# Arena places on multiples of 256 bytes in a two-batch hybrid encoder layer

## The chip, the cores and the metric

The kernel runs on one core of one Trainium2 chip. The metric is device time in microseconds (us), the median of three runs. The engines are called PE (TensorE, matmuls), PEld (its weight load), DVE (VectorE), ACT (ScalarE), POOL (GpSimd) and SP (SyncE, which here issues DMAs). SBUF addresses are bytes within one partition.

## What is computed

One encoder layer is applied to two batches with the same weights: A (1024 tokens) and B (512 tokens), 1024 channels, fp32.

```
h = RMSNorm(x);  p = h @ w_in      # q|k, v, o, z, gates | 3 x (q, k, v), z | merge gates
y_A = o * headnorm(h_fwd + h_bwd) * silu(z_A)    # mLSTM, 4 heads x 256, both directions, chunks of 128
y_B = (weighted mix of 3 dilation groups) * silu(z_B)   # 3 x 8 heads x 64, banded windows with a bias
merged = sig(g_A) * (y_A @ w_proj_m) + sig(g_B) * (y_B @ w_proj_a)
x + RMSNorm(merged @ w_out)
```

## The kernel before, in words

Every fp32 matrix is split into a high and a low part (fp32r), and a product is made of three matmuls, hi·hi (L209), hi·lo (L210) and lo·hi (L211), all in `mm3`. A dense matmul has 128 x 128 weights and 512 moving columns.

**Stage 1 (0 to 966 us)** is the input projection of A. Half blocks of h, split, lie in tiles Hh0 to Hh6 and Hl0 to Hl6; products `d` use them with weight pairs phla and phlb (`unit_pair`). The last products are the merge gates (columns `c`), which ACT writes out to gt_a. At the end the x of B (tiles xs) is normalised and turned into H (`short_input`, L313 and L319).

**Stage 2 (966 to 2260 us)** has a pool `arena` with one tile per place, taken by name with `take` (L252): H0 to H3, X0, X1, Q0, Q1, K0, K1, V0a, V0b, V1a, V1b, each 2048 fp32 per partition, the V places 2064 (eight chunks of 258: 256 values and two columns of ones). The order in which the places are first taken, the loop over names in `body`, is their order in memory. Taking a place that lies over tiles of stage 1 makes its first writer wait for their last reader. The mixer stages share the places one after another:

- mlstm of A (966 to 1312): q and k of a head in Q0/K0 or Q1/K1, v in V0a, V0b or V1a, V1b, X as work space. `ml_load` queues the loads; `fetch` (L248 to 250) issues them on SP.
- attend of A (1312 to 1640): queries in Q, keys in the V places; the `lg` matmuls (L1362, and L210/L211 in `mm3`) have 256 columns.
- mlstm of B with the combine of A beside (1640 to 1825), attend of B (1825 to 2095), combine of B and the rest (2095 to 2260).

While a mixer waits for its vector work, PE is filled with dense units of 512-column matmuls (`Fill`, in the counts STEPS): first the input projection of B (`short_units`, 768 steps), then `branches` and `final` of (A,0), (A,1) and (B,0), where the second figure is the half of the tokens. `branches` of (A,0) and (B,0) keep the split rows in V0b (hi), V1b (lo) and K0 (hi), K1 (lo): they are moving operand in `proj_m` (w_pm is the weight), are then overwritten with the merged rows by `proj_a`, and those are the weights in `final` (w_out moving). For (A,1) the same rows lie in H0 to H3, and V1b and K1 hold the attention's rows, moving operand in `proj_a`. `place` (L1569) names these places.

Weights come through a ring: a DMA into wraw (`load_w`, L261), ACT's copy to the high part (wh, L272), DVE's or POOL's difference to the low part (wl, L278). When the mixers no longer need them, X0 and Q1 serve as more of these pairs. DMAs are issued by SP in the mlstm stages and by POOL in the attend stages. The order of PE and SP in stage 2 is written out by hand; on DVE, ACT and POOL a scheduler sets it.

The gates of the mLSTM are summed into a table `gall` (128 x 128). `gate_tile` (L916) makes it, clears it on POOL, and makes the small tiles col and gb beside it. For A the table lies in a pool of stage 1; for B it lies in the pool `gates` behind the arena from the start of stage 2. B's gates are written to it (ACT, L815) while attend of A runs, and `lanes` (L934) transposes it there.

Of the kernel before, what the change touches and what calls it, by code (L numbers as in the profile page):

```python
# [22 lines left out]
F32 = mybir.dt.float32  # L23
# [6 lines left out]
P = 128  # L30
# [83 lines left out]
class Fill:  # L114
# [27 lines left out]
    def weights(self, first=True):  # L142

        if first:
            self.base = self.taken
        self.taken += 1
        self.load()
        if self.taken == len(self.ready):
            self.net.rest()
        return self.ready[self.taken - 1]  # L150
# [31 lines left out]
class Net:  # L182
# [68 lines left out]

    def take(self, name, dt=F32R, cols=2048):  # L252

        width = 2064 if name[0] == "V" else 2048
        return self.arena.tile([P, width], F32R, name=name, bufs=1)[:, :cols].bitcast(dt)

    def load_w(self, src, kt=KT, cols=P):
# [655 lines left out]

        return T.gall.rearrange("p (j r) -> p j r", r=32)[:, :, :4 * T.n].rearrange("p j (h c) -> p j h c", c=T.n)[:, :, :, t]

    def gate_tile(self, T, pool, first):  # L916
        T.gall = first.tile([P, P], F32, name=f"gall{T.S}")
        self.nc.gpsimd.memset(T.gall, 0.0)
        T.col = pool.tile([P, 3, 64], F32, name=f"col{T.S}")
        T.gb = pool.tile([P, 1], F32, name=f"gb{T.S}")  # L920
        self.nc.sync.dma_start(T.gb, self.a[f"gb{T.n}"])
# [647 lines left out]
    def place(self, which, i, dt=F32R):  # L1569

        return self.take((("V0b", "V1b", "K0", "K1"), ("H0", "H1", "H2", "H3"))[which][i], dt).rearrange("p (k t) -> p k t", k=4)
# [182 lines left out]
def body(tc, a):  # L1754
    N = Net(tc, a)
    nc = tc.nc
    (x1, y1), (x2, y2) = a["runs"]
    with ExitStack() as st:
        st.enter_context(tc.manual_schedule(engines={mybir.EngineType.PE}))
        pool = lambda name, bufs, **kw: st.enter_context(tc.tile_pool(name=name, bufs=bufs, side="left", **kw))  # L1760
        N.const = pool("const", 1)
        N.dram = dram = st.enter_context(tc.tile_pool(name="dram", bufs=1, space=DRAM))
        A = Tokens(dram, 1024, a[x1], a[y1], "a")
        B = Tokens(dram, 512, a[x2], a[y2], "b")
# [6 lines left out]
        with ExitStack() as s1:  # L1771
            hp = N.pool(s1, "H", 1, "left")
# [3 lines left out]
            with ExitStack() as sv:  # L1776
                vw = N.pool(sv, "vw", 1, "left")
                us = N.pool(s2, "us", 1, "right")
                s3, s4 = ExitStack(), ExitStack()
                begin = [vw.tile([P, 4 * VW], F32R, name=x, bufs=2) for x in ("vhi", "vlo")], *N.value_weights(vw)  # L1780
                r = [us.tile([P, 6], F32, name=f"xr{t}") for t in range(6)]
                one = us.tile([P, VW], F32, name="u2", bufs=4)[0:1, :P]
                diag = [us.tile([P, VW], F32, name="u2b", bufs=4)[:, :P] for _ in range(4)]
                xp = N.pool(s3, "x0", 1, "left"), N.pool(s4, "x1", 1, "right")
                xt = [[xp[i].tile([P, D], F32, name=f"x{i}{t}") for t in range(4)] for i in range(2)]
                minus = H[1][T4][:, 3, :P]
                spare = H[0][T4].bitcast(F32).rearrange("p a c -> p (a c)")
                row, pw = spare[0:1, D:], spare[:, :D]
                rows = lambda i, t: nc.sync.dma_start(xt[i][t], A.x[i * BLK + t * P:i * BLK + (t + 1) * P])
                weights = lambda j, kh: nc.sync.dma_start(begin[1 + j][:, kh], a["w_vp"][0, j, kh])  # L1790
                nc.scalar.dma_start(row, a["prew"][0:1])
                nc.scalar.dma_start(N.prew, a["prewc"])
                for t in range(4):
                    rows(0, t)
                weights(0, 0)
                for t in range(4):
                    rows(1, t)
                for j, kh in ((0, 1), (1, 0), (1, 1)):
                    weights(j, kh)
                nc.vector.memset(one, 1.0)  # L1800
                for i in range(2):
                    p = ps.tile([P, BLK], F32, name="d")
                    nc.tensor.matmul(p, one, row[:, i * BLK:(i + 1) * BLK], start=True, stop=True)
                    nc.vector.tensor_copy(pw[:, i * BLK:(i + 1) * BLK], p)
                nc.scalar.activation(minus, N.ident, AF.Copy, scale=-1.0)
                opened = []

                def co():
                    if not opened:
                        s4.close()  # L1810
                        opened.append(N.pool(s2, "co", 1, "right"))
                    return opened[0]

                def again():
                    H[0][T4] = place("h", T4)

                turns = N.combos(ps, H, xt, r, H[1][T4][:, :2].rearrange("p a c -> p (a c)"), pw, minus, again, diag)
                values = [N.value_group(0, A, H, vw, us, co, ps, None, (*begin, turns), [x[:, :VW] for x in xt[0]])]
                next(values[0])
                N.small(N.const)  # L1820
                N.gate_tile(A, N.const, hp)
                for _ in values[0]:
                    pass
                s3.close()
                more, turn = N.pool(sv, "more", 1, "left"), itertools.cycle(range(5))
                values += [N.value_group(g, A, H, vw, us, co, ps, late if g == 3 else None, more=more, turn=turn)
                           for g in range(1, 4)]
                next(values[1])
                with ExitStack() as s4:
                    lanes = N.lanes(A, N.pool(s4, "lane", 1, "right"), lambda: ps.tile([P, BLK], F32, name="d"))  # L1830
                    for g in range(1, 3):
                        for j, _ in enumerate(values[g]):
                            if j % 3 == 0:
                                with tc.issue_after(N.splits[0].ins), tc.issue_after(N.splits[1].ins):
                                    next(lanes, None)
                    for _ in lanes:
                        pass
                    with tc.issue_after(N.splits[0].ins):
                        N.halved()
                    N.bias_tables(N.pool(s4, "tab", 1, "right"), ps, dram)  # L1840
                for _ in range(7):
                    next(values[3])
# [63 lines left out]
        with ExitStack() as s1:  # L1906
# [4 lines left out]
            N.wsplit = [[ring.tile([P, RING], F32R, name=f"w{x}{i}") for x in "hl"] for i in range(3)]  # L1911
            N.arena = N.pool(s1, "arena", 1, "left")
            gb = N.pool(s1, "gates", 1, "left")
            N.gate_tile(B, gb, gb)
            short = N.short_units(B)
            N.last = (B, 0)
            finals = [N.final(*x) for x in ((A, 0), (A, 1), (B, 0))]
# [11 lines left out]
                end = N.short_input(N.pool(s2, "turn", 6, "right", PSUM), xt)  # L1929
            with tc.issue_after(end.ins):  # L1930
                gate(0, 6, c)
            for x in ("X0", "X1", "Q1", "K1", "V1a", "V1b", "Q0", "K0", "V0a", "V0b"):
                N.take(x)
            keep.close()
            kept = {}
# [6 lines left out]
            with ExitStack() as s2:  # L1942
                sp = N.pool(s1, "sp", 1, "right")
                N.sw = Rot(N, [sp.tile([P, BLK], F32R, name=f"sw{i}") for i in range(4)])
                N.sraw = sp.tile([P, BLK + 2], F32, name="sraw")
                nc.gpsimd.memset(N.sraw, 0.0)
                N.sg = Rot(N, [sp.tile([P, BLK], F32R, name="sg")])
                ym = N.pool(s2, "ym", 1, "right")
                N.ym_of = Rot(N, [ym.tile([P, 256], F32, name=f"ym{i}") for i in range(2)])
                N.lasting = (N.sw, N.sg, N.ym_of)  # L1950
                N.mlstm(A, fill, STEPS[0], N.ml_load(A, 0), ("a", "num", "kv"), 4,
                        hold("qkv", lambda: N.att_load(A, 0)))
                N.side = nc.gpsimd
                with ExitStack() as s3:
                    lanes = N.lanes(B, N.pool(s3, "lane2", 1, "right"), lambda: N.bank("o").rearrange("p a b -> p (a b)"))
                    N.attend(A, fill, STEPS[1], kept["qkv"], ("pt", "o", "lg"), 10, hold("head", lambda: N.ml_load(B, 0)),
                             lanes, range(44, 96, 10))
                    for _ in lanes:
                        pass
                    N.close()  # L1960
                N.side = nc.sync
                assert len(N.wsplit) == 3
                with ExitStack() as s3:
                    small = N.pool(s3, "mix", 1, "right")
                    azs = [small.tile([P, BLK], F32, name=f"az{i}") for i in range(2)]
                    beside = N.combine(A, lambda: N.ml_ps.tile([P, 4, P], F32, name="a"), ("V0b", "V1b"), ("K0", "K1"), small, azs, True)
                    N.mlstm(B, fill, STEPS[2], kept["head"], ("kv", "num", "a"), 1,
                            hold("qkv", lambda: N.att_load(B, 0)), beside)
                    for _ in beside:
                        pass  # L1970
                    N.flush(lambda p: True)
                fill.until(SHORT)
# [78 lines left out]
```

## Time and profile before

| what | value |
|---|---|
| median of 3 runs | 2256.57 us (2256.50 to 2256.66) |
| span of the profiled execution | 2259.7 us |
| granted PE clock | 1.00 |
| PE busy in mlstm A, 966 to 1312 us | 343.5 of 346 us |
| PE busy in attend A, 1312 to 1640 us | 327.8 of 328 us |
| PE busy in mlstm B, 1640 to 1825 us | 184.3 of 185 us |
| PE busy in attend B, 1825 to 2095 us | 268.5 of 270 us |
| PE busy in the rest, 2095 to 2260 us | 158.3 of 165 us |

The profiled execution lies 3.1 us above the median of the runs. In a group of instructions the columns are: line, engine, operation, output<-inputs, partitions x elements, count, then busy us in total, the mean ns of one, and the idle time before them. Buffer numbers are left out of the names, so K is K0 or K1, and wh any of the ring's high parts. A matmul's time in such a row runs from its start to its modelled end, and consecutive matmuls overlap.

### The profile page before, as it was taken

How to read it: one execution, taken by the hardware profiler on the slowest of the kernel's cores; microseconds unless marked ns; L12 is line 12 of the kernel's file. 1: busy time of each engine (PE TensorE's matmuls, PEld its weight loads, DVE VectorE, ACT ScalarE, POOL GpSimd, SP SyncE). 2: the span in 40 equal slices, each digit the busy share in tenths (PEclk: the TensorE clock that was granted, in tenths of full speed). 3: DMA queues.
4: the chain of work that ended last, by engine and by line, in shares of the span. 5: the costliest groups of instructions: out<-in, count | busy, mean ns of one | idle time of the engine just before them, and what ended most of it. 6: DMA issues, size and time to landing. Idle time of an engine off the chain costs nothing.

```text
span 2259.7 us, 35388 instructions
## 1 busy us (share of the span) xinstructions
PE 2244.2 (99%) x12226; PEld 1964.6 (87%) x12226; DVE 1509.5 (67%) x2875; ACT 1129.2 (50%) x2369; POOL 718.6 (32%) x1000
## 2 busy tenths in 40 slices
PE   9999999999999999999999999999999999999998
PEld 8999888888888888888888899999888888888887
DVE  7765577687776556558887755544689844655674
ACT  6432244344444434357777655566665644554332
POOL 1000333333333223237676610011165522221221
PEclk9999999999999999999999999999999999999999
DMA  3652455543332223284664789997678797776663
GB/s 123 168 134 76 172 205 192 192 176 121 112 111 103 84 84 140 103 298 153 226 223 127 191 217 235 253 245 221 203 248 284 238 278 211 233 251 200 233 230 109
DMA packets 222685, 418.27 MB, mean 185 GB/s; under 512 B 24841, under 2 KB 128969, under 8 KB 222506
## 3 DMA queue, kind: packets, MB, share of 16 engines
q1 hardware_dynamic: 194536, 315.86, 44.4%
q0 software_dynamic: 24368, 87.56, 12.4%
q10 hardware_dynamic: 3602, 12.59, 1.4%
q8 instruction: 97, 1.59, 0.3%
q14 instruction: 82, 0.67, 0.1%
HBM read 296.19 MB, written 128.12 MB: 188 GB/s over the span
## 4 chain that ended last, share of the span: by engine, by line
PE 95%; DMA 2%; issue 1%; ACT 1%; POOL 1%; DVE 0%; DVEq 0%; SPq 0%; POOLq 0%; ACTq 0%
PE d L211 14%; PE d L209 14%; PE d L210 14%; PE dense L209 12%; PE dense L211 12%; PE dense L210 12%; PE o L1398 4%; PE pt L1385 2%; PE lg L1362 2%; PE num L211 1%; PE num L209 1%; PE num L210 1%; PE kv L209 1%; PE a L1070 1%; PE kv L210 1%
## 5 line engine op out<-in xcount | busy, mean ns | idle before, releaser
L209 PE MATMUL dense<-H,wh 128*128 128x512 f32 x664 | 270.6, 408 | 0.8 <-DVE V0b L1643 0.8
L211 PE MATMUL dense<-H,wl 128*128 128x512 f32 x664 | 260.9, 393 | 0.0
L210 PE MATMUL dense<-H,wh 128*128 128x512 f32 x664 | 260.2, 392 | 0.0
L210 PE MATMUL d<-Hl,phla 128*128 128x512 f32 x608 | 236.5, 389 | 0.0
L211 PE MATMUL d<-Hh,phla 128*128 128x512 f32 x608 | 236.5, 389 | 0.0
L209 PE MATMUL d<-Hh,phla 128*128 128x512 f32 x608 | 236.5, 389 | 0.0
L278 DVE TENSOR_TENSOR wl<-wraw,wh 128x1024 fp32r<-128x1024 f32 (+1 forms) x121 | 149.3, 1234 | 70.0 <-ACT wh L272 69.9
L1374 DVE CUSTOM_DVE_ANT_0 ls<-lg,bias 128x256 f32<-128x256 f32 (+1 forms) x288 | 93.7, 362 | 132.8 <-PE lg L1362 71.2
L211 PE MATMUL d<-Hh,phlb 128*128 128x512 f32 x456 | 177.4, 389 | 0.0
L209 PE MATMUL d<-Hh,phlb 128*128 128x512 f32 x456 | 177.4, 389 | 0.0
L210 PE MATMUL d<-Hl,phlb 128*128 128x512 f32 x456 | 177.4, 389 | 0.0
L687 POOL TENSOR_TENSOR psum_w<-pw_raw 128x512 f32<-128x512 f32 x38 | 58.0, 1527 | 365.1 <-DMA pw_raw<-w_in 208.8
L1378 ACT ACTIVATE ls<-ls,nm 128x256 f32<-128x256 f32 (+1 forms) x288 | 130.3, 454 | 84.0 <-DVE nm L1376 59.2
L272 ACT ACTIVATE wh<-wraw 128x1024 fp32r<-128x1024 f32 (+1 forms) x124 | 128.7, 1038 | 77.1 <-PE dense L210 27.0
L211 PEld LDWEIGHTS dense<-H,wl 128*128 128x128 f32 x664 | 124.6, 188 | 28.2
L209 PE MATMUL d<-vhi,Hh 128*128 128x322 f32 x448 | 140.9, 315 | 0.3
L211 PE MATMUL d<-vhi,Hl 128*128 128x322 f32 x448 | 140.3, 313 | 0.4 <-DVE Hl L396 0.2
L210 PE MATMUL d<-vlo,Hh 128*128 128x322 f32 x448 | 139.7, 312 | 0.0
L209 PEld LDWEIGHTS dense<-H,wh 128*128 128x128 f32 x664 | 125.0, 188 | 15.5 <-DVE V0b L1643 1.2
L210 PEld LDWEIGHTS dense<-H,wh 128*128 128x128 f32 x664 | 125.4, 189 | 14.3
L211 PEld LDWEIGHTS d<-Hh,phla 128*128 128x128 f32 x608 | 114.1, 188 | 23.7
L210 PEld LDWEIGHTS d<-Hl,phla 128*128 128x128 f32 x608 | 114.2, 188 | 23.6
(570 smaller groups left out, 6166.4 us busy)
## 6 DMA issues: line engine op xcount, KB each, us to landing
pw_raw<-w_in SPq DMA_DIRECT2D x76, 512.0 KB
wraw<-w_in SPq DMA_DIRECT2D x64, 512.0 KB
aqk_a<-pwk SPq DMA_DIRECT2D x48, 512.0 KB
aqk_b<-sw SPq DMA_DIRECT2D x48, 256.0 KB
wraw<-w_pm POOLq DMA_DIRECT2D x24, 512.0 KB, 6.1
wraw<-w_out POOLq DMA_DIRECT2D x24, 512.0 KB, 4.0
wraw<-w_v POOLq DMA_DIRECT2D x22, 430.0 KB, 7.3
erep<-erow SPq DMA_DIRECT2D x16, 512.0 KB
```

The lines of the kernel that those rows point to most:

```text
L209: nc.tensor.matmul(out, lh, rh, start=start, stop=False)
L210: nc.tensor.matmul(out, lh, rl, start=False, stop=False)
L211: nc.tensor.matmul(out, ll, rh, start=False, stop=stop)
L272: high = nc.scalar.activation(hi[:, :n], raw[:, :n], AF.Copy)
L278: low = (self.lows or nc.vector).tensor_sub(lo[:, :n], raw[:, :n], hi[:, :n].bitcast(F32))
L687: self.nc.gpsimd.tensor_add(s[:, 0], ws[1][:, 0], ws[1][:, 1])
L1070: nc.tensor.matmul(p[:, c - c0], kT[:, ct, c * P:(c + 1) * P], qT[:, ct, c * P:(c + 1) * P], start=ct == 0, stop=ct == 1)
L1362: nc.tensor.matmul(lg[:, hh, c:c + w], q[hh][:, qs], z[:, k0:k0 + w], start=z is k[hh], stop=z is not k[hh])
L1374: nc.vector.tensor_tensor_reduce(out=ls[:, hh], in0=ts["lg"][hh], in1=bt[:, hh], scale=1.0, scalar=NEG, op0=OP.add, op1=OP.max, accum_out= ...
L1378: self.held = self.held[-3:] + [nc.scalar.activation(ls[:, hh], ls[:, hh], AF.Exp, bias=nm[:, hh:hh + 1], accum_out=ot[:, 128 + hh:129 + hh])]
L1385: nc.tensor.transpose(pp[:, hh * nk + x], ts["ls"][:, hh, x * P:(x + 1) * P], self.ident)
L1398: nc.tensor.matmul(po[:, hh * 64:hh * 64 + 64], pt[:, hh * nk + x], v[:, kt[x], c0 + hh * 64:c0 + hh * 64 + 64], start=x == 0, stop=x == n ...
```

## The change

The V places become 2112 fp32 wide (8448 bytes = 33 x 256), but V0b, the last, stays at 2064. The places are taken in another order: Q0 and K0 ahead of V1a and V1b. With it every place of the arena starts on a multiple of 256 bytes:

| place | before | mod 256 | after | mod 256 |
|---|---|---|---|---|
| H0 to H3, X0, X1, Q1, K1 | 50944 to 108288 | 0 | the same | 0 |
| Q0 | 132992 | 128 | 116480 | 0 |
| K0 | 141184 | 128 | 124672 | 0 |
| V1a | 116480 | 0 | 132864 | 0 |
| V1b | 124736 | 64 | 141312 | 0 |
| V0a | 149376 | 128 | 149760 | 0 |
| V0b | 157632 | 192 | 158208 | 0 |

What lies behind the arena on that side moves up by 64 bytes. So that it fits, the table gall of B leaves the pool behind the arena: it is made in a pool `sums` on the other side when attend of A starts (`gate_sums`), and is cleared there, on POOL.

```diff
     def take(self, name, dt=F32R, cols=2048):
-        width = 2064 if name[0] == "V" else 2048
+        width = 2064 if name == "V0b" else 2112 if name[0] == "V" else 2048
         return self.arena.tile([P, width], F32R, name=name, bufs=1)[:, :cols].bitcast(dt)
...
-    def gate_tile(self, T, pool, first):
-        T.gall = first.tile([P, P], F32, name=f"gall{T.S}")
+    def gate_sums(self, T, pool):
+        T.gall = pool.tile([P, P], F32, name=f"gall{T.S}")
         self.nc.gpsimd.memset(T.gall, 0.0)
+
+    def gate_tile(self, T, pool):
         T.col = pool.tile([P, 3, 64], F32, name=f"col{T.S}")
...
-                N.gate_tile(A, N.const, hp)
+                N.gate_sums(A, hp)
+                N.gate_tile(A, N.const)
...
-            N.gate_tile(B, gb, gb)
+            N.gate_tile(B, gb)
...
-            for x in ("X0", "X1", "Q1", "K1", "V1a", "V1b", "Q0", "K0", "V0a", "V0b"):
+            for x in ("X0", "X1", "Q1", "K1", "Q0", "K0", "V1a", "V1b", "V0a", "V0b"):
                 N.take(x)
...
                 with ExitStack() as s3:
+                    N.gate_sums(B, N.pool(s3, "sums", 1, "right"))
                     lanes = N.lanes(B, N.pool(s3, "lane2", 1, "right"), lambda: N.bank("o").rearrange("p a b -> p (a b)"))
```

## The prediction

> **What bounds the kernel now.** I read the page first (engine totals, clock, chain that ended last), then PE's waits from 960 us to the end, then PE's groups of instructions, shapes kept apart, in single stretches of the second stage.
>
> ```profile
> span 2259.7 us, 35388 instructions
> ...
> PE 2244.2 (99%) x12226; PEld 1964.6 (87%) x12226; DVE 1509.5 (67%) x2875; ACT 1129.2 (50%) x2369; POOL 718.6 (32%) x1000
> ...
> PEclk9999999999999999999999999999999999999999
> ...
> PE 95%; DMA 2%; issue 1%; ACT 1%; POOL 1%; DVE 0%; DVEq 0%; SPq 0%; POOLq 0%; ACTq 0%
> ```
>
> TensorE works 2244.2 of 2259.7 us, at the full granted clock in every slice, and it is 95% of the chain that ended last. So an edit can gain in two ways only: a matmul gets shorter, or one of PE's few waits goes. PE's waits in the stage that uses the arena (waiter, releaser: us in total, times, longest):
>
> ```profile
> PE num L211 <- POOL scl L1110: 1.2, 1, 1.2
> PE kv L209 <- DVE cf L1152: 1.2, 2, 0.6
> PE dense L209 <- DVE V0b L1643: 0.8, 1, 0.8
> PE dense L209 <- ACT sw L896: 0.7, 1, 0.7
> PE kv L209 <- DVE r L1163: 0.4, 1, 0.4
> ```
>
> None is released by a DMA, and these five sum to 4.3 us (the rest is 0.6). Whatever shorter or earlier loads bring, they cannot bring more than the part of these that hangs on a load (term 3 below).
>
> **What the change does to addresses.** I worked out each tile's place from the two built kernels. Before, a V tile is 2064 x 4 = 8256 bytes wide, 64 more than a multiple of 256, and every tile behind one is shifted: V1b lies at 64 mod 256, Q0, K0 and V0a at 128, V0b at 192. H0 to H3, X0, X1, Q1, K1, V1a and the weights' hi/lo tiles lie on multiples of 256 already. After, V tiles take 8448 bytes and all ten places lie on multiples of 256. The small tiles behind the arena (gates, pairs of outputs) stay off it, 64 bytes on. The instructions of PE, ACT, DVE and SP are the same in kind, number and order; one POOL memset moves, and a few first waits change. So the sum has four terms: dense matmuls, attention matmuls, the seam where the arena opens, and the memset.
>
> **Term 1: dense matmuls that touch a moved tile.** First what a matmul of 512 columns takes with nothing shifted: stage 1's d products, and two neighbours of them in time:
>
> ```profile
> L210 PE MATMUL d<-Hl,phla 128*128 128x512 f32 x608 | 236.5, 389 | 0.0
> 962.82 0.39 PE L210 MATMUL d<-Hl,phlb 128*128 128x512 f32 x1
> 965.77 0.39 PE L211 MATMUL d<-Hh,phlb 128*128 128x512 f32 x1
> ```
>
> The last column but one is the mean ns of one: 389, which holds the pipeline's depth; from 962.82 to 965.77 thirteen matmuls start, one each 227 ns, which is what a matmul costs. I take differences of the mean for differences of that pace. Now the same loop (`final`, merged rows as weights, w_out moving) in two stretches. At 2098 to 2142 the rows lie in H (unshifted):
>
> ```profile
> L211 PE MATMUL dense<-wh,H 128*128 128x512 f32 x30 | 11.7, 390 | 0.0
> L210 PE MATMUL dense<-wl,H 128*128 128x512 f32 x30 | 11.7, 389 | 0.0
> ```
>
> At 2225 to 2253 they lie in V0b/V1b (192 and 64 off) and K0/K1 (K0 128 off):
>
> ```profile
> L209 PE MATMUL dense<-wh,V0b 128*128 128x512 f32 x17 | 6.7, 394 | 0.0
> L210 PE MATMUL dense<-wl,V0b 128*128 128x512 f32 x17 | 6.7, 394 | 0.0
> L211 PE MATMUL dense<-wh,V1b 128*128 128x512 f32 x17 | 6.7, 394 | 0.0
> L210 PE MATMUL dense<-Q,K 128*128 128x512 f32 x10 | 3.9, 394 | 0.0
> L209 PE MATMUL dense<-wh,K 128*128 128x512 f32 x4 | 1.6, 392 | 0.0
> ```
>
> Same operation, same shapes, full clock: 394 against 389 to 390. Rows as moving operand, in `proj_m` (1855 to 1925, V0b/V1b and K) and `proj_a` (2064 to 2095, V1b and K1), and their unshifted peer (2000 to 2062, rows in H):
>
> ```profile
> L211 PE MATMUL dense<-V0b,wl 128*128 128x512 f32 x24 | 9.5, 396 | 0.0
> L210 PE MATMUL dense<-V1b,wh 128*128 128x512 f32 x24 | 9.4, 392 | 0.0
> L210 PE MATMUL dense<-K,wh 128*128 128x512 f32 x23 | 9.0, 390 | 0.0
> L211 PE MATMUL dense<-K,wl 128*128 128x512 f32 x22 | 8.6, 392 | 0.0
> L210 PE MATMUL dense<-K,wh 128*128 128x512 f32 x16 | 6.3, 396 | 0.0
> L211 PE MATMUL dense<-V1b,wl 128*128 128x512 f32 x16 | 6.3, 394 | 0.0
> L211 PE MATMUL dense<-H,wl 128*128 128x512 f32 x42 | 16.4, 392 | 0.0
> L210 PE MATMUL dense<-H,wh 128*128 128x512 f32 x42 | 16.4, 390 | 0.0
> ```
>
> V0b against its peer 396 to 392, V1b 392 to 390; K (half of it K1, in place already) 390 and 392, no difference; `proj_a` 396 and 394 to 390 and 392, though K1 itself is in place there: if the address is the reason, a row also shows the delay of the V1b matmul ahead of it. (Each group's first product, L209, takes in the start of a group, and its rows are left out.) The counts follow from the loops. `proj_m` runs twice here, for (A,0) and (B,0), with 8 x 8 x 3 = 192 matmuls each: 192 on V, 192 on K. The finals of the same two: 192 on V, 192 on K. `proj_a` of (A,1): 8 x 4 x 3 = 96. Together 864.
>
> - Against peers of the same stage: proj_m V 192 x 3 ns = 0.6, K 0; finals V 192 x 4 = 0.8, K 192 x 3.5 = 0.7; proj_a 96 x 4 = 0.4. Sum 2.5 us.
> - Against the pace of 389: proj_m V (394 mean) 192 x 5 = 1.0, K 192 x 2 = 0.4; finals V 192 x 5 = 1.0, K 192 x 4.5 = 0.9; proj_a 96 x 6 = 0.6. Sum 3.9 us.
>
> I take 3.3, a little above the middle: the finals, 384 of the 864, have the cleanest rows, and there both floors nearly agree. Term 1: **3.3 us (2.5 to 3.9)**. It is on the path whole, since PE never rests here.
>
> A page speaks against it. By the Trainium skill, "SBUF — State Buffer", section "Specifications (TRN2)", the SBUF's cachelines have 16 bytes; every place before is a multiple of 64, hence of 16, so by that rule term 1 would be 0. The rows disagree (394 against 389 in one loop), but they are two stages, not one stage with two addresses; the rule is rival 2.
>
> **Term 2: attention's lg matmuls** (256 columns, rows in V0a to V1b, Q):
>
> ```profile
> L1362 PE MATMUL lg<-V0b,Q 128*128 128x256 f32 x60 | 15.5, 280 | 0.0
> L1362 PE MATMUL lg<-V1a,Q 128*128 128x256 f32 x84 | 22.3, 317 | 0.0
> L211 PE MATMUL lg<-V0a,Q 128*128 128x256 f32 x32 | 9.0, 282 | 0.0
> L210 PE MATMUL lg<-V1b,Q 128*128 128x256 f32 x16 | 4.4, 278 | 0.0
> ```
>
> V1a is in place before and still shows 317: these groups have another limit, and moving a place gives them nothing. For the flat ones (L1362 about 288, L210/L211 about 128, 416 in all), no unshifted row of this shape exists. Half a 512-column matmul's pace is 113 ns, so 389 - 113 = 276 is the floor: 4 ns at most, 1.7 us. The other end is 0, since 278 already stands beside tiles 64 off. I take the middle, **0.8 us (0 to 1.7)**.
>
> **Term 3: the seam.** Where stage 1's half-block tiles end and the arena opens, a place waits for what it covers. Q0 and K0 move down by 16.5 KB, V1a and V1b up. SP's queue before (issue time, duration), then the chain of waits up to PE's longest wait:
>
> ```profile
> 966.91 0.80 SPq L250 DMA_DIRECT2D Q<-qk_a  x2
> 967.81 0.87 SPq L250 DMA_DIRECT2D K<-qk_a  x2
> 972.35 8.28 DMA gt_a<-c
> 980.70 6.48 DMA wraw<-w_in
> 990.46 6.51 DMA rw<-rw_a
> 998.25 0.46 POOL scl L1110
> 998.76 0.39 PE num L211
> ```
>
> Q0's first load waits before for the last DVE operation of the last product (ends 966.89); after, for a PE matmul of an earlier product on a stage-1 tile, by the order at 962.8 to 963.2. It can start 3.7 us sooner. K0's load waits for the end of the last products' matmuls (966.0), so it moves 1 to 1.7 us, and the rw, V0a and V0b loads queued behind it on SP with it. They run beside gt_a<-c, which takes 8.28 us and holds back the weight load at 980.70; with one load gone ahead, I expect it 1 to 2 us sooner. That passes down the chain to rw, POOL's scl and the 1.2 us that PE waits at 998.76. More than the wait itself can't be won; nothing is won if ACT, which has other work before 987, is late next. I take **0.9 us (0 to 1.2)**. The reverse, Q's transfer ahead of the write taking bandwidth from it, needs 8.28 to grow by over a microsecond though the same bytes run earlier; I give it no term, only the room above the range's middle.
>
> **Term 4: the memset** of the gate sums' table goes from ahead of stage 2 to the start of attention of A, on POOL, just ahead of l_one:
>
> ```profile
> 1309.13 0.20 POOL L950 MEMSET l_one<- 64x128 f32 x1
> 1317.53 0.63 POOL L261 DMA_DIRECT2D wraw<-w_v  x1 [8.05 <-DVE wl L278]
> ```
>
> One more of 0.20 us; behind it POOL idles 8.05 us, which hides it. ACT's first gate copy and PE's transpose of the table now wait for it, long after it is done. Without that cover it would delay one weight load by 0.2 us; I put **0**, both ways. Loads into the moved tiles and the DVE, ACT and POOL operations on them I put at 0 too: PE waits for no load, and its other waits are for chains of small tiles that don't move.
>
> **Sum.** 3.3 + 0.8 + 0.9 = 5.0 us (2.5 to 6.8). Span 2259.7 - 5.0 = 2254.7. The profiled execution lies 3.1 us above the median of the runs (2259.7 to 2256.57), so the runs come to **2251.6** (2249.8 to 2254.1).
>
> **Rivals.**
> 1. Only part of the offset counts. After, V0b and V1b lie on even multiples of 256, while H, X0, X1 and the weights, the tiles of the 389 rows, lie on odd ones. If the period is 512, V's share of term 1 (0.6 + 0.8 at least) and half of term 2 stay. Left: 1.3 (K, proj_a) + 0.4 + 0.9 = 2.6, 2254.0. For it: no row shows a tile at an even multiple. Against: K0 at 128 shows no loss in proj_m, so a finer rule is as likely. Chance 0.16.
> 2. The address doesn't matter; 394 belongs to those stages (more DMA into the ring, DVE writing m2 beside). Then the change doesn't do what it says, and the seam alone is left: 2256.6 - 0.9 = 2255.7. For it: H shows 392 in one stage and 389 in the next; the 16-byte rule named above. Against: two finals with the same loads differ by 4 to 5 ns throughout. Chance 0.17.
> 3. Slower: with all places in one phase of 256, two streams that PE reads at once (weights of the next matmul, rows of this one) meet in the same place of the memory, and each of the 864 loses instead of gains. The price: V0b's 396 in proj_m, the highest flat row, is 7 over the pace; if the finals and projections all went from 394 to 402, 864 x 8 = 6.9, less 0.9: 2262.6. It decides from 864 x 6 ns on (5.4 - 0.9 = 4.5 us). Against: H, ring and phla share that phase now and give the fastest rows, 389. Chance 0.04.
> 4. More than the sum: the same offsets also cost in groups that look bound by something else (lg at 317). One ns in each of 3000 matmuls is 3 us: 2248.6. Chance 0.05.
>
> **How the numbers follow.** The forecast has 0.58; the rest is as above. A measurement tells 0.2% from no change, 4.5 us: faster means under 2252.06. The forecast's own spread lies about 0.7 under that line and 0.3 over it (0.41 and 0.17). Rivals 1 and 2 count as same, 3 as slower, 4 as faster. Faster 0.46, same 0.50, slower 0.04. The range goes from 2249.4 to 2255.9: it takes in rivals 1 and 2, and leaves out 3, 4 and the forecast's outer edge.
>
> **What would show it.** Right: in the finals of (A,0) and (B,0), the V0b, V1b and K rows at 389 to 390; V0b in proj_m at 392; the wait num<-scl at 0.3 or less, Q<-qk_a issued near 963; lg flat rows at 276 to 278. Rival 1: K falls, V0b and V1b stay at 394. Rival 2: all stay. Rival 3: the rows rise above 394. What would make the whole wrong is a new PE wait on a load or on an ACT or DVE chain that now ends late, which no row of before shows, or a difference in the part of stage 1 that the change doesn't touch.

## The result, and the profile after

The changed kernel runs in 2253.72 us (median of 21 runs, 2251.40 to 2257.87), beside 2256.92 for the kernel before on the same chips (21 runs, 2256.35 to 2260.09). The ratio is 0.9981, 95% interval 0.9976 to 0.9987: 4.3 us faster (2.9 to 5.4). A second timing of the same kernel, in another session (e6 below), gave 0.9976 (0.9966 to 0.9986).

The page of the profile after, and all of PE's waits in it:

```profile
span 2250.7 us, 35392 instructions
...
PE 2238.9 (99%) x12226; PEld 1964.4 (87%) x12226; DVE 1510.2 (67%) x2875; ACT 1128.0 (50%) x2369; POOL 713.5 (32%) x1000
```

```profile
PE d L1805 <- DMA Hh<-prew: 2.4, 1, 2.4
PE d L391 <- DVE u2b L389: 0.7, 1, 0.7
PE kv L209 <- DVE cf L1154: 0.6, 1, 0.6
PE d L438 <- ACT Hh L432: 0.5, 1, 0.5
PE dense L210 <- DVE Q L278: 0.3, 1, 0.3
PE d L211 <- DVE Hl L396: 0.2, 1, 0.2
PE kv L209 <- DVE cf L1151: 0.2, 1, 0.2
PE d L211 <- DVE Hl L434: 0.2, 1, 0.2
```

PE's busy time fell by 5.3 us, and num<-scl is gone from the list of waits. The two spans differ by 9.0 us, twice what the runs say. The runs of after state why: its profiled execution has a span of 2250.7 and a time of 2252.45, 1.75 apart. With the same 1.75, the profiled execution of before, span 2259.7, took about 2261.4, nearly 5 us over its own median: it was a late one. Its waits dense<-V0b (0.8) and dense<-sw (0.7) are absent from e1's profile below, of practically the same kernel. So waits are compared here across several profiles; groups of matmuls that wait for nothing repeat to some tenths of a ns (last section) and can be compared directly.

The final of (B,0) in after, 2222 to 2248 us, and two rows of `proj_m` of (A,0), 1847 to 1917:

```profile
L209 PE MATMUL dense<-wh,V0b 128*128 128x512 f32 x15 | 5.8, 389 | 0.0
L210 PE MATMUL dense<-wl,V0b 128*128 128x512 f32 x15 | 5.8, 389 | 0.0
L211 PE MATMUL dense<-wh,V1b 128*128 128x512 f32 x15 | 5.8, 389 | 0.0
L210 PE MATMUL dense<-Q,K 128*128 128x512 f32 x8 | 3.1, 389 | 0.0
```

```profile
L211 PE MATMUL dense<-V0b,wl 128*128 128x512 f32 x23 | 9.0, 390 | 0.0
L210 PE MATMUL dense<-V1b,wh 128*128 128x512 f32 x23 | 9.0, 390 | 0.0
```

Every row of the final stands at 389, where those that the prediction shows stood at 392 to 394; V0b in proj_m went from 396 to 390. The attention's lg matmuls went the other way, from 280 to 282 (groups of the whole span):

```profile
L1364 PE MATMUL lg<-V0b,Q 128*128 128x256 f32 x60 | 15.6, 282 | 0.0
L1364 PE MATMUL lg<-V1b,Q 128*128 128x256 f32 x60 | 15.6, 282 | 0.0
```

SP's queue at the seam, and POOL's where the memset went (start, duration):

```profile
962.42 0.80 SPq L250 DMA_DIRECT2D Q<-qk_a  x2
965.14 0.80 SPq L250 DMA_DIRECT2D K<-qk_a  x2
965.99 0.90 SPq L250 DMA_DIRECT2D rw<-rw_a  x2
```

```profile
1304.82 0.20 POOL L918 MEMSET gall<- 128x128 f32 x1
1304.97 0.20 POOL L952 MEMSET l_one<- 64x128 f32 x1
1305.11 0.20 POOL L953 MEMSET l_zero<- 64x128 f32 x1
1313.24 0.63 POOL L261 DMA_DIRECT2D wraw<-w_v  x1 [7.94 <-DVE wl L278]
```

Stage 1 ran 0.8 us earlier in this profile, so Q's load moved by 4.5 - 0.8 = 3.7 us through the change, as worked out, and K's by 2.7 - 0.8 = 1.9, a little more than the 1 to 1.7 expected; the memset fills idle time.

For the rest I use two measures worked out from the traces. **Flat** is the sum, over all PE matmuls from 966 us on that neither wait nor stand next to one that waits, of the difference to before in the time from start to next start. After: -3.2 us (1825 to the end -3.3, attend of A +0.5, the rest -0.3). **Pace** is the mean time from start to next start of 512-column matmuls within stretches in which the places of both operands mod 256 stay the same; the first six and the last three matmuls of a stretch are left out.

### The profile page after: what moved, and what is told of

Same layout as the page of the kernel before. It is cut to its first block, busy times and chain, and to the rows that moved or that the text cites. A ratio compares the mean times of both kernels' runs of the same rounds, so it can differ in the third digit from the quotient of the medians.

```text
span 2250.7 us, 35392 instructions
## 1 busy us (share of the span) xinstructions
PE 2238.9 (99%) x12226; PEld 1964.4 (87%) x12226; DVE 1510.2 (67%) x2875; ACT 1128.0 (50%) x2369; POOL 713.5 (32%) x1000
## 4 chain that ended last, share of the span: by engine, by line
PE 97%; issue 1%; DMA 1%; DVE 0%; ACT 0%; POOL 0%; DVEq 0%; POOLq 0%; ACTq 0%
PE d L211 14%; PE d L209 14%; PE d L210 14%; PE dense L209 12%; PE dense L211 12%; PE dense L210 12%; PE o L1400 4%; PE pt L1387 2%; PE lg L1364 2%; PE num L209 1%; PE num L211 1%; PE num L210 1%; PE a L1072 1%; PE kv L209 1%; PE kv L210 1%
## 5 line engine op out<-in xcount | busy, mean ns | idle before, releaser
L211 PE MATMUL dense<-H,wl 128*128 128x512 f32 x664 | 260.6, 393 | 0.0
L210 PE MATMUL dense<-H,wh 128*128 128x512 f32 x664 | 260.4, 392 | 0.0
L210 PE MATMUL d<-Hl,phla 128*128 128x512 f32 x608 | 236.5, 389 | 0.0
L211 PE MATMUL d<-Hh,phla 128*128 128x512 f32 x608 | 236.5, 389 | 0.0
L278 DVE TENSOR_TENSOR wl<-wraw,wh 128x1024 fp32r<-128x1024 f32 (+1 forms) x121 | 149.5, 1236 | 66.4 <-ACT wh L272 66.3
L211 PE MATMUL d<-Hh,phlb 128*128 128x512 f32 x456 | 177.4, 389 | 0.0
L210 PE MATMUL d<-Hl,phlb 128*128 128x512 f32 x456 | 177.4, 389 | 0.0
L211 PEld LDWEIGHTS dense<-H,wl 128*128 128x128 f32 x664 | 124.7, 188 | 28.1
L209 PE MATMUL d<-vhi,Hh 128*128 128x322 f32 x448 | 140.9, 314 | 0.3
L211 PE MATMUL d<-vhi,Hl 128*128 128x322 f32 x448 | 140.3, 313 | 0.4 <-DVE Hl L396 0.2
L210 PE MATMUL d<-vlo,Hh 128*128 128x322 f32 x448 | 139.6, 312 | 0.0
L210 PEld LDWEIGHTS dense<-H,wh 128*128 128x128 f32 x664 | 125.3, 189 | 14.3
L210 PEld LDWEIGHTS d<-Hl,phla 128*128 128x128 f32 x608 | 114.1, 188 | 23.7
```

The source lines that it names most:

```text
L209: nc.tensor.matmul(out, lh, rh, start=start, stop=False)
L210: nc.tensor.matmul(out, lh, rl, start=False, stop=False)
L211: nc.tensor.matmul(out, ll, rh, start=False, stop=stop)
L278: low = (self.lows or nc.vector).tensor_sub(lo[:, :n], raw[:, :n], hi[:, :n].bitcast(F32))
```

## The experiments

All eleven keep every engine's instructions in the order of after. "Single address" is the reason that the prediction gave: an operand off a multiple of 256 costs. "Stage" is its rival 2.

**e1: the table alone.** After with the old order and the old width:

```diff
-        width = 2064 if name == "V0b" else 2112 if name[0] == "V" else 2048
+        width = 2064 if name[0] == "V" else 2048
-            for x in ("X0", "X1", "Q1", "K1", "Q0", "K0", "V1a", "V1b", "V0a", "V0b"):
+            for x in ("X0", "X1", "Q1", "K1", "V1a", "V1b", "Q0", "K0", "V0a", "V0b"):
```

> The kernel before with only the gate sums' table moved; places and widths as before. Address theory (a 512-column matmul with an operand off a multiple of 256 bytes takes 2 to 6 ns more, and the seam gives about 1 us): as before, within 1 us; rows of the last final (B,0) at 392 to 395, PE's wait num<-scl near 1.2 us. Stage theory (the address is nothing, only the earlier loads at the seam count): the same. If the table's move itself gave time: 2 us or more under before. It also shows which of the small PE waits of the profile of before come again.

Measured: ratio 1.0001 (0.9993 to 1.0010), flat -0.2. The table's move gives nothing. Its waits from 960 us on, and rows of its final of (B,0) at 2222 to 2248:

```profile
PE num L211 <- POOL scl L1112: 1.0, 1, 1.0
PE kv L209 <- DVE r L1165: 0.4, 1, 0.4
PE dense L210 <- DVE Q L278: 0.2, 1, 0.2
```

```profile
L209 PE MATMUL dense<-wh,V0b 128*128 128x512 f32 x16 | 6.3, 394 | 0.0
L210 PE MATMUL dense<-Q,K 128*128 128x512 f32 x9 | 3.5, 394 | 0.0
```

num<-scl and the slow rows belong to the layout; dense<-V0b and dense<-sw came and went.

**e2: wide tiles, old order.** After with only the list of names put back (second pair of lines above).

> The changed kernel with the places in the old order but the wide V tiles: all ten on multiples of 256, Q0 and K0 high up as before. Address theory: about 3.5 us under before (term 1 whole, no seam): 2253.4; last final's rows all at 389, the wait num<-scl back at about 1.2 us. Stage theory: as before, 2256.9, rows 392 to 395.

Measured: ratio 0.9978 (0.9969 to 0.9986), flat -3.2, all rows of the last final at 389, num<-scl at 1.2:

```profile
L209 PE MATMUL dense<-wh,V0b 128*128 128x512 f32 x16 | 6.2, 389 | 0.0
L210 PE MATMUL dense<-Q,K 128*128 128x512 f32 x10 | 3.9, 389 | 0.0
```

The stage theory is out: same stages, same seam, other places, and the matmuls are short. The gain of the kernel is there without the new order.

**e3: new order, old width.** After with only the width put back (first pair of lines).

> The changed kernel with the new order but the old width of V: Q0, K0, V1a on multiples of 256, V1b at 64, V0a at 128, V0b at 192. Address theory: K's part of term 1 and the seam, 1.1 + 1.2 = 2.3 us under before: 2254.6; in the last final the K rows at 389, the V0b and V1b rows at 394. Stage theory: the seam alone, 1.2 us under before, 2255.7, with K and V rows alike.

Measured: ratio 0.9993 (0.9984 to 1.0002), flat -0.5. The single address expected K at 389 and V at 394; the last final has:

```profile
L210 PE MATMUL dense<-wl,V0b 128*128 128x512 f32 x16 | 6.3, 396 | 0.0
...
L210 PE MATMUL dense<-Q,K 128*128 128x512 f32 x8 | 3.1, 392 | 0.0
```

K is in place and still not at 389, and the L210 row of V0b rose from 394 (before) to 396. In the trace the first three matmuls after a change from V to K keep the slow pace, which spoils half of each group of six K matmuls. Where the V tiles lie at different places, putting K right gave almost nothing.

**e4: the whole arena 64 bytes on.**

```diff
-            N.wsplit = [[ring.tile([P, RING], F32R, name=f"w{x}{i}") for x in "hl"] for i in range(3)]
+            N.wsplit = [[ring.tile([P, RING + 16 * (x + str(i) == "l2")], F32R, name=f"w{x}{i}")[:, :RING] for x in "hl"] for i in range(3)]
```

> The changed kernel with the whole arena 64 bytes further (a wider last weight tile of the ring ahead of it), so that all ten places and H0 to H3, X0, X1, Q1, K1, V1a lie at 64 mod 256, with the same order of instructions; the ring's weights stay in place. Address theory: some 2850 dense matmuls touch a place, at 3 to 5 ns each 8.5 to 14 us more than the changed kernel, so 2262 to 2268, and all rows of final (A,1), in H, rise from 389 to 393 or more. Stage theory: as the changed kernel, 2253.7 (2255 if the seam is lost, since places then cover two tiles of stage 1).

Measured: ratio 1.0002 (0.9993 to 1.0011), flat +0.8: slower than after, so places matter, but by 4.0 us of flat, where the single address expected 8.5 to 14. The trace shows why. PE's starts in the final of (B,0):

```profile
2214.92 0.39 PE L209 MATMUL dense<-wh,V0b 128*128 128x512 f32 x1
...
2217.72 0.39 PE L209 MATMUL dense<-X,V0b 128*128 128x512 f32 x1
...
2219.10 0.39 PE L209 MATMUL dense<-Q,K 128*128 128x512 f32 x1
...
2220.46 0.39 PE L209 MATMUL dense<-wh,V0b 128*128 128x512 f32 x1
```

From 2214.92 to 2217.72 the ring's weight (at 0) streams against V and K (at 64): twelve matmuls, 233 ns each. From 2219.10 to 2220.46 Q streams against K, both at 64: six matmuls, 227 each. Two operands off by the same 64 bytes cost nothing. (The six matmuls from 2217.72 to 2219.10, X against V at the same 64, took 230 in the mean: 226, 235, 229, 232, 231 and 227 in turn. Behind the ring's slow group the second to the fifth are still late.) The theory that I formed from this: **what counts is where the two operands lie relative to each other, mod 256.**

**e5: ring and arena both 64 bytes on.** After with the second raw tile of the ring 16 columns wider, ahead of the weights, so that all tiles behind it move alike.

```diff
-            N.wraw = [ring.tile([P, RING], F32, name=f"wraw{i}") for i in range(2)]
+            N.wraw = [ring.tile([P, RING + 16 * i], F32, name=f"wraw{i}")[:, :RING] for i in range(2)]
```

> The changed kernel with the weights' tiles of the ring (hi and lo) and the whole arena 64 bytes further, so that both operands of every dense matmul of stage 2 lie at 64 mod 256. Theory of the single address (each operand off 256 costs): at least as slow as e4_shift64, so the time of the kernel before or above it; rows of the finals at 394 or more. Theory of the relative phase (what costs is that the moving operand and the weights lie at different places mod 256, as e4's rows suggest, where Q as moving operand with K as weights, both at 64, kept the pace of 389): all rows of the finals at 389, 4 to 5 us under before, as the changed kernel.

Measured: ratio 0.9984 (0.9975 to 0.9992), flat -2.6, and in the last final, where nothing lies on a multiple of 256:

```profile
L209 PE MATMUL dense<-wh,V0b 128*128 128x512 f32 x16 | 6.2, 389 | 0.0
L210 PE MATMUL dense<-wl,V0b 128*128 128x512 f32 x16 | 6.2, 389 | 0.0
L211 PE MATMUL dense<-wh,V1b 128*128 128x512 f32 x16 | 6.2, 389 | 0.0
L210 PE MATMUL dense<-Q,K 128*128 128x512 f32 x9 | 3.5, 389 | 0.0
```

The single address has fallen, the relative one holds. Flat gained 0.6 less than in after, of which 0.4 is in attend of A; why is not traced. In attend of A one lg matmul waited for a load, which no profile of after shows:

```profile
PE lg L1364 <- DMA V0b<-aqk_a: 0.2, 1, 0.2
```

The other lg matmuls of e5 that follow three of their kind kept 119.5 ns (119.9 in after), so this is no effect of the place.

**e6: after once more**, beside e5.

> The changed kernel once more, beside e5_all64 on the same chip: both theories 0.9975 to 0.999 of before. Its waits, against those of the first profile, show which of PE's small waits come and go from one execution to the next.

Measured: 0.9976, flat -3.2; no wait num<-scl, and dense<-V0b absent again, while e5 beside it had it at 1.1.

**e7 to e10: other distances.** As e4 with 8, 24, 32 and 48 columns in place of 16; e9 and e10 also have the old width of V, to fit.

> The changed kernel with the arena at 32 mod 256, the ring at 0. For the size of the step. If the cost grows with the distance: rows of final (A,1) at 391 to 393 where H at 32 is the weight and the ring at 0 moves (64 gave about 396). If only lines of 64 bytes or more count: 389. Theory of the single address: the same rows, but also Q and X as moving operand with H, both at 32, above 389; relative phase: those at 389.

> The changed kernel with the arena at 96 mod 256, the ring at 0: the same question at three times the distance. Growing with distance: 396 or more for ring against arena, weights H; a plateau: the 396 of 64. Relative phase: Q and X against H at 389.

> Arena at 128 mod 256 and ring at 0, with V tiles of the old width so that it fits (V0a then lies at 0, V0b at 64, V1b at 192): H, X, Q and K are 128 from the ring. Final (A,1), H as weights against the ring: if the pattern repeats every 128 bytes, 389; if every 256, 394 to 396 as at 32, 64 and 96. X and Q against H, both at 128: 389 by the relative phase.

> The same with the arena at 192 and the ring at 0. In e4 (arena 64) weights 64 ahead of the moving operand cost 6.6 ns and weights 64 behind it only 2. With a period of 256, 192 is 64 the other way round: final (A,1) against the ring at about 391, proj with H moving against the ring's weights at about 395. With a period of 512 or more, no such exchange.

Measured, one run each: 2263.24 and 2262.20 (before, beside them, 2258.80), 2260.79 and 2263.15 (before 2259.14); flat +6.1, +6.3, +3.6, +5.3. Final (A,1), ring against H, at 2100 to 2130 us of e7, e8, e9 and e10:

```profile
L210 PE MATMUL dense<-wl,H 128*128 128x512 f32 x23 | 9.1, 395 | 0.0
```

```profile
L210 PE MATMUL dense<-wl,H 128*128 128x512 f32 x23 | 9.1, 396 | 0.0
```

```profile
L210 PE MATMUL dense<-wl,H 128*128 128x512 f32 x22 | 8.7, 393 | 0.0
```

```profile
L210 PE MATMUL dense<-wl,H 128*128 128x512 f32 x22 | 8.6, 392 | 0.0
```

Already 32 bytes cost the full price, so it doesn't grow with distance. The paces of all these traces, by the place of the moving operand less that of the weights, mod 256 (number of matmuls):

| distance | pace, ns | from |
|---|---|---|
| 0 (both at 0, 32, 64, 96, 128 or 192) | 227.0 to 227.8 | all kernels |
| 32 | 233.4 (453) | e7 |
| 64 | 228.9 (447), 228.9 (15) | e4, e10 |
| 96 | 233.5 (460) | e8 |
| 128 | 232.8 (288), 233.5 (15) | e9 |
| 160 | 233.9 (42) | e8 |
| 192 | 233.3 (42), 233.3 (279) | e4, e10 |
| 224 | 233.1 (42) | e7 |

e4 and e10 give the same two values with the operands exchanged, so 64 and 192 are each other's reverse, as a period of 256 demands; 128 still costs, so the period isn't 128. V0b and V1b at even multiples of 256 beside a ring at odd ones run at 389 in after, so it isn't 512.

**e11: the value weights of stage 1.** Their 1344 matmuls of 322 columns move slices of 1288 bytes, whose places run through 0 to 120 mod 256 against H at 0. After with

```diff
-        place = lambda: [sb.tile([P, N], F32R, name=x, bufs=2) for x in ("vhi", "vlo")]
+        place = lambda: [sb.tile([P, N + 24], F32R, name=x, bufs=2)[:, :N] for x in ("vhi", "vlo")]
-                begin = [vw.tile([P, 4 * VW], F32R, name=x, bufs=2) for x in ("vhi", "vlo")], *N.value_weights(vw)
+                begin = [vw.tile([P, 4 * VW + 24], F32R, name=x, bufs=2)[:, :4 * VW] for x in ("vhi", "vlo")], *N.value_weights(vw)
```

> The changed kernel with the value weights of stage 1 (vhi, vlo, four slices of 322 columns each, 1288 bytes) padded by 96 bytes per tile: the tiles start at 0 and 128 mod 256 in place of 0, 32, 64 and 96, hi and lo of a pair alike. They are moving operand of 1344 matmuls against H at 0. If the phase matters there as for 512 columns: the mean of these matmuls (312 to 315) moves by 1 to 3 ns, up to 1.3 to 4 us, either way, since no phase stays 0 through the slices. If these are held by something else: no change beside the changed kernel's 2253.5 (0.9976 to 0.9981 of before).

Measured: 2250.71 us, ratio 0.9962 (0.9948 to 0.9975), the fastest of all. Rows of after, then of e11:

```profile
L211 PE MATMUL d<-vhi,Hl 128*128 128x322 f32 x448 | 140.3, 313 | 0.4 <-DVE Hl L396 0.2 <-DVE Hl L434 0.2
L210 PE MATMUL d<-vlo,Hh 128*128 128x322 f32 x448 | 139.6, 312 | 0.0
```

```profile
L211 PE MATMUL d<-vhi,Hl 128*128 128x322 f32 x448 | 138.8, 310 | 0.4 <-DVE Hl L396 0.2 <-DVE Hl L434 0.2
L210 PE MATMUL d<-vlo,Hh 128*128 128x322 f32 x448 | 138.7, 310 | 0.0
```

These two and the third (140.9 to 140.7) sum to 2.6 us; the mean from start to next start fell from 150.7 to 148.6 ns. The trace of after shows the slowest places of this shape: slices at 32 and 40 mod 256 took 155.3 ns, all others 149.5 in the mean, and e11 has no slice at these two. Which places are best was not mapped; these were one choice that fits. After was not timed beside e11, so what e11 gains over it in measured time is known less well than the rows.

## Why the prediction was right, and where it was wrong

- **The bound** held: PE's matmuls and its few waits; no load mattered.
- **Term 1** (3.3 us) was right in size: flat from 1825 us on, where these matmuls run, fell by 3.3, and the 864 matmuls alone by 3.2 (proj_m V 0.8 and K 0.3, finals V 0.9 and K 0.8, proj_a 0.5, each rounded). Of the two floors, 389 was the better one for the finals: their rows went all the way to it.
- **Its reason failed.** The step "every tile behind a V tile is shifted", with H's 389 as the unshifted row, compared tiles that were also in step with the ring. The dense rows of before held only pairs in which one operand was at 0, so they could not tell "off a multiple" from "off each other". e4 and e5 did. That the wrong reason had no price is luck: the places were moved onto multiples of 256, and the ring lay on them already, so that all came into step. The row that was noted as odd (K1 in place, 396) fits: a group in step stays slow for three matmuls behind one out of step, and K1 stood between V1b's.
- **Term 2** (0.8 gain) had the wrong sign: lg lost 0.4 us of flat, in after, e2, e6 and e11 alike (0.3 of the 0.5 in attend of A, and 0.1 later). The step that failed is the floor: half of 227 ns. In after 256 columns, in lg matmuls that follow three of their kind, take 119.9 ns and 512 take 227; the difference is 107 for 256 columns. On a straight line through these two some 13 ns don't shrink with the width, an estimate, and 276 was no floor. e8 (117.4 ns) and e7 (120.4) have lg's operands in step too, so its pace follows places in a way that the table doesn't give.
- **Term 3** (0.9): num<-scl fell from 1.0 or 1.2 us with the old order (before, e1, e2) to 0 in after and e6, so in the trace it is right; but it kept 0.6 in e3, and with the arena at 64 it was 0 in e4 and 1.2 in e5, so the chain seems to be only just in time. The weight load of 980.70 was issued at 978.72, 2.0 - 0.8 = 1.2 us sooner through the change, as expected. In measured time the term could not be seen: e2, without the gain, and after, with it, have the same ratio within their intervals.
- **Term 4** was 0, as e1 shows.
- **The sum** by the traces is 3.3 - 0.5 + 1.1 = 3.9, and 0.3 from elsewhere in flat makes 4.2, beside 4.3 measured and 5.0 forecast. It should not be taken to be as exact as it looks: by the same sum e2, without the seam, gains 3.2, and it measured 0.9978, 5.0 us (3.2 to 7.0). The offset of 3.1 us between execution and median was a mistake of reading: span and time differ, and the execution was late. It did no harm, since the sum was taken off both.
- **Rival 1** (period 512) and **rival 2** (stage) are out by the 389 rows of V0b/V1b in after and by e2. **Rival 3** had the right object, the two streams that PE reads at once, and the wrong direction: in step they are fast, out of step slow. Why is not shown; no run looked below the paces.
- The section of the Trainium skill's page "SBUF — State Buffer", "Specifications (TRN2)", with its cachelines of 16 bytes, doesn't cover this: distances of 32 and more, all multiples of 16, cost 5 to 7 ns in 227 (64 alone 2).

Open: why distance 64 is nearly free, why lg and 322 columns have other best places, and why dense<-wl,V0b took 233.9 ns in the mixed triples of before, with V0b at 192 and V1b at 64, where a uniform stretch at its distance, 64, takes 228.9. Open too is which weights count. In the profiles each matmul's weights load while the one before it runs (before: the L211 matmul of 2235.57 has its weight load at 2235.34, beside the L210 matmul of 2235.33); in a uniform stretch both lie at the same place, so the paces can't tell whether the moving operand has to be in step with its own weights or with those that load meanwhile. The prediction's rival 3 had the second in mind, and no run parted the two.

## What to carry to other kernels

Where PE is busy for the whole span, look at which bytes its two operands start on: on this chip, in 512-column fp32r matmuls, both at the same place mod 256 ran at 227 ns and apart at 229 to 234, and padding a V tile cost 192 bytes per partition here. Put the weights' ring and every place that it is multiplied with in step, all of them: one place put right among wrong ones gave little (e3). When one row is compared with another in a trace, ask in which respects the two differ; a variant that moves both operands tells what one that moves a single operand can't.

## What the runs showed of the hardware

- The pace of a matmul depends on the relative place of its operands mod 256 bytes, by up to 3%, and repeats to 0.2 ns between executions (e1 and before: 233.8 and 233.9 for dense<-wl,V0b).
- The effect of a group out of step lasts into the next group, in step: three matmuls behind V in e3 (233, 233, 230, then 227), up to the fifth behind the ring's group in e4 (226, 235, 229, 232, 231, then 227).
- DVE, ACT and POOL showed nothing of the kind: with all arena places moved in e4, e5 and e7 to e10, and the value tiles in e11, DVE was busy for 1504 to 1510 us (before 1509.5), ACT for 1127 to 1128 (before 1129.2) and POOL for 713 to 719 (before 718.6), in no order of the distances.
